# Split weights kept in DRAM from the first segment on, and a head's maximum as one row made by transposes

## The chip, the cores and the metric

The kernel runs on one core of one Trainium2 chip. The metric is the device time of one execution in microseconds, from the profiled execution and from runs timed without a profile. TensorE appears in the views as PE (matmuls) and PEld (weight loads), VectorE as DVE, ScalarE as ACT, GpSimd as POOL; a `q` behind an engine's name is its queue, from which it also issues transfers. SP is the queue that issues most of them. Sixteen DMA engines move the data.

## The reference

Two consecutive layers of a decoder trunk over 2048 tokens of width 1024, in float32. Both layers begin with an RMS norm, shifted and scaled by a condition vector, and end with a projection, a gate and a residual sum.

- Layer 0 projects to 3072 columns: four heads of a gated linear recurrence (key 128, value 128) and a causal pooling mixer with windows of 2, 4, 8 and 16, each with its own SiLU gate, then an output projection.
- Layer 1 projects to 4 x 1024 + 16 columns: queries, keys, values and gate of 16 heads of 64, and one forget logit a head. Queries and keys are RMS normed. The attention is causal with a bias of cumulative log forget values:

```
logits = q @ k.T * 64**-0.5 + cumf[:, q, None] - cumf[:, None, k]
probs  = softmax(where(causal, logits, -inf))
o      = (probs @ v) * silu(g);   x = x + gate * (o @ w_out)
```

## The kernel before

**Segments.** The 2048 tokens go in four segments of 512 (`SEG`), each through layer 0 and then layer 1, so that keys and values of earlier segments ("past chunks") are read back from DRAM. A segment has a projection stretch (layer 0, its output projection, the first projections of layer 1) and an attention stretch (16 heads, with the rest of the projections woven between).

**Precision by splitting.** A float32 operand of a matmul is split into a rounded part (type fp32r) and the remainder, and a product takes three passes (`PASSES`): high x high, high x low, low x high.

**Weights.** A weight tile is 1024 x 256. `wseq` lists the order of their use: 12 tiles of kind `a` (layer 0 in), 4 of `b` (layer 0 out), 16 of `c` (layer 1 in) and 4 of `d` (layer 1 out) in each segment, 144 uses in all, and one last tile `e` put together from parts of `d`. `prep_w(n)` loads a tile in four quarters `raw` of 256 KB (four buffers), casts each into the high half of `wt` on ACT (line 293) and subtracts into the low half, on POOL or on DVE in turn (line 294, helper line 182). This is done at every use. `wt` has two buffers, and `next_w` prepares the tile behind the one that it hands out.

**Attention operands.** For head h `prep` makes `Q1`, `Q3`, `K1` and `K2` from the transposed projection. `K1` (128 rows) holds the low and the high half of the keys. `K2` has 68 rows: 64 rows of the high half of the keys, two rows of the forget bias (high and low, from `cfd`), and two rows of ones. `Q3` has 68 rows that face these: 64 rows of queries, two of ones, and two that hold the negated maximum of each query, high and low; they begin as zeros (from `q4d`). For later segments `K1` and `K2` are stored to `k1d` and `k2d` (lines 1080 and 1081), values to `vd`.

**Maximum pass and attention.** `max_pass(s, h)` multiplies `Q3` with every chunk of `K2` and takes the maximum of each query. Past chunks come by `old_k2`, a load of 68 rows of 512 columns on SP's queue into one of three buffers (`k2o`, line 1086). At its end the maximum, four columns of 128, is negated and split by small DVE operations into eight columns (`mhl`), transposed at once to 8 rows, copied to `mr` and brought by a transfer on ACT's queue into rows 66 and 67 of `Q3` (line 1118), since a row that spans 512 columns is wanted there. `attend(s, h)` then computes, for each block of 128 keys, `pst` from `K1`, `Q1` and from `K2`, `Q3`, its exponential `ph`, the remainder `pl`, and the products with the values (`pov`, `pol`). It loads every past chunk's `K1o`, `K2o` and `Vo` itself. So every past chunk's `K2` is loaded twice for a head: once by the maximum pass, once by attention.

**Order.** `quad_attention` runs the steps of `attend` for head h in turn with those of `max_pass` for head h + 1, and calls `prep` for head h + 2 behind them; `weave` puts steps of the remaining projections (`quad_fill`) between. Instructions are put on the engines' queues by priority, which follows the program's order, and each queue runs in its order. In `prep_w` casts and subtractions are put back by 80 in priority.

Of the kernel before, what the change touches and what calls it, by code (L numbers as in the profile page):

```python
# [8 lines left out]
F32 = mybir.dt.float32  # L9
F32R = mybir.dt.float32r  # L10
BF16 = mybir.dt.bfloat16
U8 = mybir.dt.uint8
AF = mybir.ActivationFunctionType
ALU = mybir.AluOpType
# [4 lines left out]
P = 128  # L19
T = 2048  # L20
D = 1024
ND = D // P
SEG = 512
NSEG = T // SEG
NTB = SEG // P
NH = 16
HD = 64
VW = 2 * HD + 2
EPS = 1e-6
NEG = -1e30  # L30

# [2 lines left out]
def trunk(ctx, tc, x, cvec, norm_g, ada_c, ada_w, ada_b, ada_bg, lbp, w0, w0o, w1, w1f, w1o,  # L34
          onorm, poolw, pscale, foxb, qkg, out):
    nc = tc.nc
    V, S, G = nc.vector, nc.scalar, nc.gpsimd

    def mm(*a, **k):
        return nc.tensor.matmul(*a, **k)  # L40

    def transpose(o, i):
        return nc.tensor.transpose(o, i, ident[0:i.shape[0], 0:i.shape[0]])
# [5 lines left out]
    wp = E(tc.tile_pool(name="wp", bufs=2))  # L49
# [4 lines left out]
    sp = E(tc.tile_pool(name="sp", bufs=2))  # L54
    ps = E(tc.tile_pool(name="ps", bufs=2, space=PSUM))
    dr = E(tc.tile_pool(name="dr", bufs=1, space=DRAM))
# [6 lines left out]
    def small(shape, name, dt=F32):  # L63
        return sp.tile(shape, dt, name=name, tag=name)
# [22 lines left out]
    def f(ap):  # L87
        return ap.bitcast(F32)
# [32 lines left out]
    for lv in range(NL):  # L121
        half = 1 << lv
        b = 2 * half
# [26 lines left out]

    x1d = dr.tile([T, D], F32, name="x1d")
    k1d = dr.tile([NH, P, T], F32, name="k1d")
    k2d = dr.tile([NH, HD + 4, T], F32, name="k2d")
    vd = dr.tile([NH, P, T // P, VW], F32, name="vd")
    cfd = dr.tile([NH, 4, T], F32, name="cfd")
    q4d = dr.tile([4, SEG], F32, name="q4d")
    gd = dr.tile([2, D], F32, name="gd")


    def rsqrt_mean(out_t, ss, n, name):  # L160
# [101 lines left out]
    wseq = []  # L262
# [8 lines left out]
    wsrc = {"a": w0, "b": w0o, "c": w1, "d": w1o}  # L271
    grow1 = []
    wready = {}
    wpos = [0]

    def prep_w(n):
        if n >= len(wseq) or n in wready:
            return
        late = wseq[n][0] == "e"
        src = None if late else wsrc[wseq[n][0]][wseq[n][1]]  # L280
        wt = wp.tile([P, 2, ND, 256], F32R, name="wt", tag="wt")
        parts = range(3 if late else 4)
        if not late and n >= len(wseq) - 5:
            parts = range((NEARLY[wseq[n][1]] + 1) // 2)
        for h in parts:
            sl = slice(2 * h, 2 * h + 2)
            raw = wp.tile([P, 2, 256], F32, name="raw", tag="raw", bufs=4)
            nc.sync.dma_start(raw, w1o[h][:, ND - 2:, :] if late else src[:, sl, :])
            if late:
                V.tensor_tensor(raw, raw, grow1[0][:, h * 256:(h + 1) * 256].unsqueeze(1).to_broadcast([P, 2, 256]),  # L290
                                op=ALU.mult)
            tc.cur_priority += 80
            S.copy(wt[:, 0, sl, :], raw)  # L293
            split_lo(wt[:, 1, sl, :], raw, wt[:, 0, sl, :], G if (h % 2 or n == 0) and n < len(wseq) - 2 else V)
            tc.cur_priority -= 80
        wready[n] = wt

    def next_w(key, ahead=True):
# [611 lines left out]
    NEARLY = (6, 7, 7, 8)  # L910
# [65 lines left out]
    def forget_rows(s, act):  # L976
        pf = ps_pj("pfl")

        for d in range(ND):
            for b in range(2):  # L980
                mm(pf[0:48, :], wf[:, d, :], act[:, d, b, :], start=(d + b == 0), stop=(d + b == ND))
        z = tmp("z")[0:NH]
        S.activation(z, pf[0:NH, :], AF.Identity, bias=fb)
        V.tensor_tensor(z, pf[32:32 + NH, :], z, op=ALU.add)
        a = tmp("za")[0:NH]
        S.activation(a, z, AF.Abs)
        S.activation(a, a, AF.Exp, scale=-1.0)
        S.activation(a, a, AF.Ln, bias=1.0)

        V.scalar_tensor_tensor(z, z, 0.0, a, op0=ALU.min, op1=ALU.subtract)  # L990
        cf = tmp("cf")[0:NH]
        V.tensor_tensor_scan(cf, z, zero1[0:NH].to_broadcast([NH, SEG]), fcar, op0=ALU.add, op1=ALU.add)
        V.tensor_copy(fcar, cf[:, SEG - 1:SEG])
        V.tensor_scalar(cf, cf, -1.0, None, op0=ALU.mult)
        ch_ = tmp("cfh", F32R)[0:NH]
        V.tensor_copy(ch_, cf)
        cl = tmp("cfl", F32R)[0:NH]
        split_lo(cl, cf, ch_)
        nc.sync.dma_start(cfd[:, 0, s * SEG:(s + 1) * SEG], f(ch_))
        nc.sync.dma_start(cfd[:, 1, s * SEG:(s + 1) * SEG], f(cl))  # L1000

    seg1 = [dict() for _ in range(NSEG)]

# [53 lines left out]
    def prep(s, h):  # L1057

        L = seg1[s]
        qk = L["qk", h // 2]  # L1060
        j = h % 2
        pt = ps_misc("pqkT")
        for tb in range(NTB):
            transpose(pt[:, tb * P:(tb + 1) * P], qk[:, tb, j * P:(j + 1) * P])
        lo, up = slice(0, HD), slice(HD, P)
        g = col["qkg"]
        Q1 = qp.tile([P, SEG], F32R, name="Q1", tag="qa")
        Q3 = qp.tile([P, SEG], F32R, name="Q3", tag="qb")
        K1 = kp.tile([P, SEG], F32R, name="K1", tag="k1c")
        K2 = kp.tile([P, SEG], F32R, name="K2", tag="k2c")  # L1070
        S.activation(Q1[lo], pt[lo], AF.Copy, scale=g[lo])
        S.activation(K1[up], pt[up], AF.Copy, scale=g[up])
        V.scalar_tensor_tensor(Q1[up], pt[lo], g[lo], f(Q1[lo]), op0=ALU.mult, op1=ALU.subtract)
        V.scalar_tensor_tensor(K1[lo], pt[up], g[up], f(K1[up]), op0=ALU.mult, op1=ALU.subtract)
        S.copy(Q3[lo], f(Q1[lo]))
        S.copy(K2[lo], f(K1[up]))
        nc.scalar.dma_start(f(Q3[HD:HD + 4]), q4d)
        nc.scalar.dma_start(f(K2[HD:HD + 4]), cfd[h, :, s * SEG:(s + 1) * SEG])
        if s < NSEG - 1:
            nc.sync.dma_start(k1d[h, :, s * SEG:(s + 1) * SEG], f(K1))  # L1080
            nc.sync.dma_start(k2d[h, :, s * SEG:(s + 1) * SEG], f(K2[0:HD + 4]))
        L["ops", h] = (Q1, Q3, K1, K2)

    def old_k2(h, c):
        K2 = kp.tile([P, SEG], F32R, name="K2o", tag="k2o", bufs=3)
        nc.sync.dma_start(f(K2[0:HD + 4]), k2d[h, :, c * SEG:(c + 1) * SEG])
        return K2

    def max_pass(s, h):

        _, Q3, _, K2 = seg1[s]["ops", h]
        mxs = small([P, NTB, NSEG], "mxs")
        for c in range(s + 1):
            kc = K2 if c == s else old_k2(h, c)
            for i in range(NTB):
                n = SEG if c < s else (i + 1) * P
                pm = ps_mx("pmx")
                mm(pm[:, 0:n], Q3[0:HD + 4, i * P:(i + 1) * P], kc[0:HD + 4, 0:n], start=True, stop=True)
                if c < s:
                    V.tensor_reduce(mxs[:, i, c:c + 1], pm[:, 0:n], axis=AX.X, op=ALU.max)  # L1100
                else:
                    V.tensor_tensor_reduce(pm[:, 0:n], pm[:, 0:n], mq[:, SEG - n:], 1.0, NEG, op0=ALU.add,
                                           op1=ALU.max, accum_out=mxs[:, i, c:c + 1])
                if c < s or i < NTB - 1:
                    yield
        m = small([P, NTB], "m")
        V.tensor_reduce(m, mxs[:, :, 0:s + 1], axis=AX.X, op=ALU.max)
        mhl = small([P, 2, NTB], "mhl")
        mh = small([P, NTB], "mh", F32R)
        V.tensor_scalar(mh, m, -1.0, None, op0=ALU.mult)  # L1110
        V.tensor_copy(mhl[:, 0, :], f(mh))
        V.scalar_tensor_tensor(mhl[:, 1, :], m, -1.0, f(mh), op0=ALU.mult, op1=ALU.subtract)
        yield
        pt = ps_misc("pmt")
        transpose(pt[0:2 * NTB, 0:P], mhl.rearrange("p a b -> p (a b)"))
        mr = sp.tile([2 * NTB, P], F32R, name="mr", tag="mr", bufs=1)
        V.tensor_copy(mr, pt[0:2 * NTB, 0:P])
        nc.scalar.dma_start(f(Q3[HD + 2:HD + 4].rearrange("a (b t) -> a b t", t=P)), f(mr))

    def attend(s, h):  # L1120

# [2 lines left out]
        Q1, Q3, K1, K2 = L["ops", h]  # L1124
# [14 lines left out]
        for c in range(s + 1):  # L1139
            if c < s:  # L1140
                k1 = kp.tile([P, SEG], F32R, name="K1o", tag="k1o", bufs=2)
                nc.sync.dma_start(f(k1), k1d[h, :, c * SEG:(c + 1) * SEG])
                k2 = old_k2(h, c)
                vv = kp.tile([P, NTB, VW], F32R, name="Vo", tag="vo", bufs=2)
                nc.sync.dma_start(f(vv), vd[h, :, c * NTB:(c + 1) * NTB, :])
            else:
                k1, k2, vv = K1, K2, vc[:, :, j, :]
            for b in range(NTB):
                q0 = 0 if c < s else b * P
                ks = slice(b * P, (b + 1) * P)  # L1150
                st = ps_st("pst")
                mm(st[:, q0:], k1[:, ks], Q1[:, q0:], start=True, stop=False)
                mm(st[:, q0:], k2[0:HD + 4, ks], Q3[0:HD + 4, q0:], start=False, stop=(c < s))
                if c == s:
                    mm(st[:, q0:q0 + P], identb, mk, start=False, stop=True)
                ph = tmp("ph", F32R)
# [125 lines left out]
    def constants():  # L1282
# [15 lines left out]
        V.memset(o1, 1.0)  # L1298
        z1 = tmp("z1")
        V.memset(z1, 0.0)  # L1300
        nc.sync.dma_start(q4d[0:2, :], o1[0:2])
        nc.sync.dma_start(q4d[2:4, :], z1[0:2])
        for s in range(NSEG):
            nc.sync.dma_start(cfd[:, 2, s * SEG:(s + 1) * SEG], o1[0:NH])
            nc.sync.dma_start(cfd[:, 3, s * SEG:(s + 1) * SEG], o1[0:NH])
        wfr = tmp("wfr", F32, (P, ND, NH))
        nc.sync.dma_start(wfr, w1f)
        V.tensor_copy(wf[:, :, 0:NH], wfr)
# [80 lines left out]
```

## Time and profile before

| | |
|---|---|
| median of 3 runs | 3062.76 us (3058.55 to 3068.89) |
| the profiled execution | 3059.16 us |
| its span, first to last instruction | 3057.4 us |
| PE busy / DVE / ACT / POOL | 2799.8 / 2373.8 / 1792.8 / 1191.7 us |
| bytes moved by DMA | 338.56 MB, 111 GB/s in the mean |
| attention stretches | 345 to 690, 955 to 1386, 1665 to 2190, 2455 to 3041 us |

The table's times of engines are busy times over the whole span; they overlap. The stretches are given from the start of the span, and were read from the first and last matmuls of attention. The 1.8 us between span and execution lie around the first and last instruction.

### The profile page before, as it was taken

To read this page: it belongs to the slowest core of one execution; us is meant where nothing else is said; L and a number is where in the kernel's file an instruction comes from. 1 tells how busy PE (TensorE), PEld (TensorE's weight loads), DVE (VectorE), ACT (ScalarE), POOL (GpSimd) and SP (SyncE) were. 2 spreads that over 40 slices of the span, in tenths; PEclk is the share of its full clock that TensorE was granted. 3 is DMA by queue.
4 is the path that set the end of the run, shared out by engine and by line. 5 is a ranking of instruction groups with operands and counts; after the bars stand their busy time and mean duration, and the time that the engine had idled before them with its cause. 6 is when DMAs were issued, how large, how long until landed. Compare 5 with 4: busy or idle time off the path is not lost.

```text
span 3057.4 us, 49147 instructions
## 1 busy us (share of the span) xinstructions
PE 2799.8 (92%) x17020; PEld 2378.7 (78%) x17020; DVE 2373.8 (78%) x4646; ACT 1792.8 (59%) x3679; POOL 1191.7 (39%) x992
## 2 busy tenths in 40 slices
PE   4999898999998898999999899989999999999998
PEld 4888877879887777779888677777888977676767
DVE  8877688867676888876677888888758688888886
ACT  3454566763545666674445666667544566666674
POOL 3321233323212444434111555554421246655565
PEclk9999999999999999999999999999999999999999
DMA  6423454424234334434234343443333323333342
GB/s 247 163 78 104 120 141 106 122 77 128 73 114 111 101 96 109 130 90 135 68 102 118 111 108 115 117 125 106 115 99 94 110 90 101 103 96 99 92 135 79
DMA packets 198904, 338.56 MB, mean 111 GB/s; under 512 B 19768, under 2 KB 67000, under 8 KB 196096
## 3 DMA queue, kind: packets, MB, share of 16 engines
q1 hardware_dynamic: 195264, 321.52, 36.3%
q10 hardware_dynamic: 3392, 13.90, 1.3%
q8 instruction: 135, 2.21, 0.3%
q14 instruction: 113, 0.93, 0.1%
HBM read 285.72 MB, written 49.36 MB: 110 GB/s over the span
## 4 chain that ended last, share of the span: by engine, by line
PE 49%; DVE 16%; DMA 6%; ACT 5%; issue 3%; POOL 0%; SPq 0%; DVEq 0%; ACTq 0%; POOLq 0%
PE py L40 9%; PE pst L40 6%; PE pgt L40 6%; PE pqk L40 6%; PE pv L40 4%; PE pmx L40 3%; DMA K2o<-k2d 3%; PE pov L40 3%; PE pol L40 2%; PE pq L40 2%; DVE pl L182 2%; PE pl L40 2%; PE pf L40 2%; DVE wt L182 2%; DMA Q<-mr 2%
## 5 line engine op out<-in xcount | busy, mean ns | idle before, releaser
L182 POOL TENSOR_TENSOR wt<-raw,wt 128x512 fp32r<-128x512 f32 x287 | 431.3, 1511 | 998.1 <-ACT wt L293 931.9
L1168 POOL TENSOR_TENSOR la<-la,ph 128x512 f32<-128x512 f32 (+3 forms) x528 | 614.6, 1164 | 445.4 <-ACT ph L1157 396.5
L1157 ACT ACTIVATE ph<-pst 128x512 fp32r<-128x512 f32 (+3 forms) x640 | 341.6, 534 | 277.6 <-PE pst L40 258.6
L182 DVE TENSOR_TENSOR pl<-pst,ph 128x512 fp32r<-128x512 f32 (+3 forms) x640 | 385.7, 604 | 123.2 <-ACT pst L1158 111.1
L40 PE MATMUL pqk<-wt,h 128*128 128x256 f32 x3072 | 457.4, 286 | 5.7 <-DVE h L495 2.6
L40 PEld LDWEIGHTS pqk<-wt,h 128*128 128x128 f32 x3072 | 426.4, 192 | 29.8 <-DVE h L495 3.4
L40 PE MATMUL pgt<-h,wt 128*128 128x512 f32 x1536 | 418.5, 406 | 0.2 <-ACT e L527 0.2
L293 ACT CAST wt<-raw 128x512 fp32r<-128x512 f32 x578 | 337.3, 622 | 72.2 <-PE py L40 33.3
L40 PE MATMUL pv<-wt,h 128*128 128x256 f32 x2304 | 346.9, 295 | 6.0 <-DVE h L182 4.3
L40 PEld LDWEIGHTS pv<-wt,h 128*128 128x128 f32 x2304 | 324.1, 200 | 22.7 <-DVE h L182 6.4
L1158 ACT ACTIVATE pst<-pst 128x512 f32<-128x512 f32 (+3 forms) x640 | 340.1, 531 | 0.0
L40 PEld LDWEIGHTS pgt<-h,wt 128*128 128x128 f32 x1536 | 290.4, 194 | 62.0 <-issue 1.9
L182 DVE TENSOR_TENSOR wt<-raw,wt 128x512 fp32r<-128x512 f32 x291 | 264.2, 912 | 54.7 <-ACT wt L293 53.2
L1100 DVE TENSOR_REDUCE mxs<-pmx 128x1 f32<-128x512 f32 x384 | 258.4, 685 | 46.9 <-PE pmx L40 43.4
L40 PE MATMUL py<-wt,o 128*128 128x256 f32 x1536 | 203.6, 287 | 1.3 <-ACT o L1204 1.2
L40 PE MATMUL py<-wt,mix 128*128 128x256 f32 x1536 | 198.4, 287 | 3.0 <-DVE yt L842 2.1
L40 PEld LDWEIGHTS py<-wt,o 128*128 128x128 f32 x1536 | 194.2, 193 | 7.0 <-ACT o L1204 1.5
L40 PEld LDWEIGHTS py<-wt,mix 128*128 128x128 f32 x1536 | 187.7, 191 | 10.7 <-issue 4.5
L40 PE MATMUL pst<-Q,K2o 68*128 68x512 f32 x384 | 150.2, 412 | 39.6 <-DMA Q<-mr 23.0
L40 PE MATMUL pst<-Q,K1o 128*128 128x512 f32 x384 | 161.9, 427 | 18.8 <-DVE pl L182 18.2
L40 PE MATMUL pov<-ph,Vo 128*128 128x512 f32 x384 | 164.5, 428 | 4.4 <-ACT ph L1157 2.9
L40 PE MATMUL pst<-Q,K 128*128 128x512 f32 (+7 forms) x512 | 131.8, 335 | 37.1 <-DVE pl L182 27.9
(254 smaller groups left out, 5307.4 us busy)
## 6 DMA issues: line engine op xcount, KB each, us to landing
raw<-in_w_dram SPq DMA_DIRECT2D x448, 256.0 KB
K2o<-k2d SPq DMA_DIRECT2D x192, 136.0 KB
Vo<-vd SPq DMA_DIRECT2D x96, 260.0 KB
K1o<-k1d SPq DMA_DIRECT2D x96, 256.0 KB
raw<-in_w1o_dram SPq DMA_DIRECT2D x66, 256.0 KB
raw<-in_w0o_dram SPq DMA_DIRECT2D x64, 256.0 KB
vd<-Vc SPq DMA_DIRECT2D x48, 260.0 KB
ada<-in_ada_w_dram ACTq DMA_DIRECT2D x12, 1024.0 KB
```

What stands on the lines that cost most here:

```text
L40: return nc.tensor.matmul(*a, **k)
L182: (eng or V).tensor_tensor(out_t, full, f(hi), op=ALU.subtract)
L293: S.copy(wt[:, 0, sl, :], raw)
L1100: V.tensor_reduce(mxs[:, i, c:c + 1], pm[:, 0:n], axis=AX.X, op=ALU.max)
L1157: S.activation(ph[:, q0:], st[:, q0:], AF.Exp)
L1158: S.activation(st[:, q0:], st[:, q0:], AF.Exp)
L1168: G.tensor_tensor(la[:, q0:], la[:, q0:], f(ph[:, q0:]), op=ALU.add)
```

## The change

Two things are changed.

The first use of a weight tile, in the first segment, is as before, and the finished tile (high and low half, 2.1 MB) is then stored to a DRAM tensor `wd` by a transfer on ACT's queue. Every later use loads both halves from there into `wt`, 1 MB each, on SP's queue; the casts and subtractions are left out. The last uses of `d` load only the parts that are used (`NEARLY`).

The maximum of a head is no longer split into two rows. Its four columns are transposed one by one into one row of 512 columns in PSUM, and ACT writes the negated row into `Q3`. `Q3` and `K2` have 67 rows (`KR`) in place of 68: the row of the maximum (a row of ones in `K2`) stands first, the two rows of the bias behind it. `k2d`, `cfd` and `q4d` change their shape with it.

```diff
+KR = HD + 3
...
-    k2d = dr.tile([NH, HD + 4, T], F32, name="k2d")
+    k2d = dr.tile([NH, KR, T], F32, name="k2d")
...
-    cfd = dr.tile([NH, 4, T], F32, name="cfd")
-    q4d = dr.tile([4, SEG], F32, name="q4d")
+    cfd = dr.tile([NH, 3, T], F32, name="cfd")
+    q4d = dr.tile([3, SEG], F32, name="q4d")
...
+    wd = {k: dr.tile([n, P, 2, ND, 256], F32, name="wd" + k) for k, n in (("a", 12), ("b", 4), ("c", 16), ("d", 4))}
...
+        if not late and wseq[n] in wsplit:
+            kind, i = wseq[n]
+            wt = wp.tile([P, 2, ND, 256], F32R, name="wt", tag="wt")
+            nd = NEARLY[i] if n >= len(wseq) - 5 else ND
+            for b in range(2):
+                nc.sync.dma_start(f(wt[:, b, 0:nd, :]), wd[kind][i, :, b, 0:nd, :])
+            wready[n] = wt
+            return
...
-        if not late and n >= len(wseq) - 5:
-            parts = range((NEARLY[wseq[n][1]] + 1) // 2)
...
+        if not late:
+            wsplit.add(wseq[n])
+            nc.scalar.dma_start(wd[wseq[n][0]][wseq[n][1]], f(wt))
...
-        nc.scalar.dma_start(f(Q3[HD:HD + 4]), q4d)
-        nc.scalar.dma_start(f(K2[HD:HD + 4]), cfd[h, :, s * SEG:(s + 1) * SEG])
+        nc.scalar.dma_start(f(Q3[HD:KR]), q4d)
+        nc.scalar.dma_start(f(K2[HD:KR]), cfd[h, :, s * SEG:(s + 1) * SEG])
...
-            nc.sync.dma_start(k2d[h, :, s * SEG:(s + 1) * SEG], f(K2[0:HD + 4]))
+            nc.sync.dma_start(k2d[h, :, s * SEG:(s + 1) * SEG], f(K2[0:KR]))
...
-        nc.sync.dma_start(f(K2[0:HD + 4]), k2d[h, :, c * SEG:(c + 1) * SEG])
+        nc.sync.dma_start(f(K2[0:KR]), k2d[h, :, c * SEG:(c + 1) * SEG])
...
-                mm(pm[:, 0:n], Q3[0:HD + 4, i * P:(i + 1) * P], kc[0:HD + 4, 0:n], start=True, stop=True)
+                mm(pm[:, 0:n], Q3[0:KR, i * P:(i + 1) * P], kc[0:KR, 0:n], start=True, stop=True)
...
-        mhl = small([P, 2, NTB], "mhl")
-        mh = small([P, NTB], "mh", F32R)
-        V.tensor_scalar(mh, m, -1.0, None, op0=ALU.mult)
-        V.tensor_copy(mhl[:, 0, :], f(mh))
-        V.scalar_tensor_tensor(mhl[:, 1, :], m, -1.0, f(mh), op0=ALU.mult, op1=ALU.subtract)
         yield
         pt = ps_misc("pmt")
-        transpose(pt[0:2 * NTB, 0:P], mhl.rearrange("p a b -> p (a b)"))
-        mr = sp.tile([2 * NTB, P], F32R, name="mr", tag="mr", bufs=1)
-        V.tensor_copy(mr, pt[0:2 * NTB, 0:P])
-        nc.scalar.dma_start(f(Q3[HD + 2:HD + 4].rearrange("a (b t) -> a b t", t=P)), f(mr))
+        for i in range(NTB):
+            transpose(pt[0:1, i * P:(i + 1) * P], m[:, i:i + 1])
+        S.activation(Q3[HD:HD + 1], pt[0:1], AF.Copy, scale=-1.0)
...
-                mm(st[:, q0:], k2[0:HD + 4, ks], Q3[0:HD + 4, q0:], start=False, stop=(c < s))
+                mm(st[:, q0:], k2[0:KR, ks], Q3[0:KR, q0:], start=False, stop=(c < s))
```

The constant rows of `cfd` and `q4d`, written once at the start, move with the rows: three rows in place of four, and four stores fewer.

## Rows read from the trace of the kernel before

**Rows 1.** The page, busy us (share of the span) and instructions of each engine.
```profile
PE 2799.8 (92%) x17020; PEld 2378.7 (78%) x17020; DVE 2373.8 (78%) x4646; ACT 1792.8 (59%) x3679; POOL 1191.7 (39%) x992
```
**Rows 2.** The page, the chain of waits that ended last, by line.
```profile
PE py L40 9%; PE pst L40 6%; PE pgt L40 6%; PE pqk L40 6%; PE pv L40 4%; PE pmx L40 3%; DMA K2o<-k2d 3%; PE pov L40 3%; PE pol L40 2%; PE pq L40 2%; DVE pl L182 2%; PE pl L40 2%; PE pf L40 2%; DVE wt L182 2%; DMA Q<-mr 2%
```
**Rows 3.** Stages: stretch and its us, busy us by engine, PE's clock, DMA share, GB/s.
```profile
345.00:690.00 345.00, 312.54 (x2018) 270.77 (x2017) 268.90 (x578) 222.67 (x467) 106.76 (x105) 0.98 0.42 112
690.00:955.00 265.00, 255.86 (x1760) 231.55 (x1758) 183.87 (x359) 125.60 (x263) 67.18 (x48) 0.99 0.36 108
955.00:1386.00 431.00, 385.82 (x2255) 320.99 (x2256) 346.12 (x683) 280.20 (x580) 176.60 (x153) 0.96 0.40 106
...
1665.00:2190.00 525.00, 474.65 (x2631) 383.86 (x2630) 432.00 (x825) 355.72 (x721) 268.36 (x218) 0.98 0.40 112
...
2455.00:3041.00 586.00, 540.08 (x2924) 428.62 (x2923) 497.28 (x903) 390.86 (x774) 343.47 (x280) 0.98 0.33 99
```
**Rows 4.** Transfers issued in the last attention stretch, 2455 to 3041: count, KB each.
```profile
K2o<-k2d SPq DMA_DIRECT2D x93, 136.0 KB
raw<-in_w_dram SPq DMA_DIRECT2D x48, 256.0 KB
...
raw<-in_w1o_dram SPq DMA_DIRECT2D x18, 256.0 KB
```
**Rows 5.** Transfers issued in the third attention stretch, 1665 to 2190.
```profile
raw<-in_w_dram SPq DMA_DIRECT2D x64, 256.0 KB
K2o<-k2d SPq DMA_DIRECT2D x64, 136.0 KB
...
k2d<-K SPq DMA_DIRECT2D x16, 136.0 KB
```
**Rows 6.** Transfers in the second, 955 to 1386; its raw and k2d counts equal rows 5's.
```profile
K2o<-k2d SPq DMA_DIRECT2D x32, 136.0 KB
```
**Rows 7.** SP's queue in order of time: start us, us of the issue.
```profile
2616.19 0.33 SPq L1142 DMA_DIRECT2D K1o<-k1d  x1
2616.61 0.66 SPq L1086 DMA_DIRECT2D K2o<-k2d  x2
...
2624.04 0.25 SPq L1086 DMA_DIRECT2D K2o<-k2d  x1
2626.99 0.34 SPq L1142 DMA_DIRECT2D K1o<-k1d  x1
```
**Rows 8.** Two short stretches behind such issues, columns as in rows 3.
```profile
2617.50:2618.00 0.50, 0.50 (x4) 0.40 (x3) 0.49 (x2) 0.50 (x2) 0.50 (x1) 1.00 0.97 295
...
2625.34:2626.34 1.00, 1.00 (x6) 0.69 (x5) 0.73 (x2) 0.77 (x2) 0.57 (x2) 1.00 0.25 98
```
**Rows 9.** A stretch in which PE waits and the one behind it, columns as rows 3.
```profile
1000.30:1003.70 3.40, 0.73 (x4) 0.46 (x5) 3.33 (x5) 1.49 (x3) 1.99 (x2) 1.00 0.64 172
1003.80:1007.00 3.20, 3.20 (x11) 2.51 (x11) 1.66 (x3) 1.06 (x2) 0.00 (x0) 0.50 0.19 71
```
**Rows 10.** Groups of instructions on the weights: busy us, mean ns, idle before.
```profile
L182 POOL TENSOR_TENSOR wt<-raw,wt 128x512 fp32r<-128x512 f32 x287 | 431.3, 1511 | 998.1 <-ACT wt L293 931.9 <-DVE pl L182 24.3 <-DMA raw<-in_w_dram 16.2
...
L293 ACT CAST wt<-raw 128x512 fp32r<-128x512 f32 x578 | 337.3, 622 | 72.2 <-PE py L40 33.3 <-issue 9.1 <-DMA raw<-in_w_dram 8.5
...
L182 DVE TENSOR_TENSOR wt<-raw,wt 128x512 fp32r<-128x512 f32 x291 | 264.2, 912 | 54.7 <-ACT wt L293 53.2
```
**Rows 11.** Groups around the maximum row, and ACT's copy of the same length.
```profile
L1179 ACT COPY u<-pov 64x512 f32<-64x512 f32 x64 | 37.3, 583 | 33.7 <-PE pov L40 27.8 <-PE pol L40 3.0 <-DVE o L182 1.1
L1110 DVE TENSOR_SCALAR mh<-m 128x4 fp32r<-128x4 f32 x64 | 25.5, 398 | 0.9
```
**Rows 12.** Who waited for whom, whole span: us in total, times, longest us.
```profile
PE pst L40 <- DVE pl L182: 46.1, 61, 3.4
...
PE pst L40 <- DMA Q<-mr: 30.9, 14, 6.3
...
PE pst L40 <- DMA K2o<-k2d: 16.4, 19, 2.0
```

More of the change, by code (lines that the diff above doesn't have):

```diff
@@ L273, in trunk @@
     wready = {}
+    wsplit = set()
     wpos = [0]
@@ L998, in forget_rows @@
         split_lo(cl, cf, ch_)
-        nc.sync.dma_start(cfd[:, 0, s * SEG:(s + 1) * SEG], f(ch_))
-        nc.sync.dma_start(cfd[:, 1, s * SEG:(s + 1) * SEG], f(cl))
+        nc.sync.dma_start(cfd[:, 1, s * SEG:(s + 1) * SEG], f(ch_))
+        nc.sync.dma_start(cfd[:, 2, s * SEG:(s + 1) * SEG], f(cl))
     seg1 = [dict() for _ in range(NSEG)]
@@ L1300, in constants @@
         V.memset(z1, 0.0)
-        nc.sync.dma_start(q4d[0:2, :], o1[0:2])
-        nc.sync.dma_start(q4d[2:4, :], z1[0:2])
+        nc.sync.dma_start(q4d[1:3, :], o1[0:2])
+        nc.sync.dma_start(q4d[0:1, :], z1[0:1])
         for s in range(NSEG):
-            nc.sync.dma_start(cfd[:, 2, s * SEG:(s + 1) * SEG], o1[0:NH])
-            nc.sync.dma_start(cfd[:, 3, s * SEG:(s + 1) * SEG], o1[0:NH])
+            nc.sync.dma_start(cfd[:, 0, s * SEG:(s + 1) * SEG], o1[0:NH])
         wfr = tmp("wfr", F32, (P, ND, NH))
```

## The prediction

> **What bounds the kernel now.** Read first the share of busy time of each engine: TensorE (PE) is busy 92% of the span, so anything that shortens other engines can give back at most the rest [rows 1]. The chain of waits says the same in another way: its largest pieces are matmuls, but two transfers stand in it, the old key rows `K2o` (3%) and the maximum row `mr` (2%) [rows 2]. An average over the run hides where the room is, so the third view is the table by stage: a projection stretch has PE busy 255.86 of 265.00 us, while the four attention stretches leave 32 to 50 us each [rows 3]. In the projections only PE matters. In attention PE waits for others, and the loads of old keys are among those others. So the fourth view is the list of transfers in the attention stretches: each `K2o` load is 136 KB, 68 rows of 2 KB, and there are 93, 64 and 32 of them in the last three stretches, with 16 stores `k2d<-K` of the same shape in the middle ones [rows 4, 5, 6].
>
> The fifth view decides: how wide such a transfer runs. The load issued at 2624.04 is alone in flight until the next issue at 2626.99 [rows 7]. In the microsecond inside it the DMA engines are 0.25 busy and move 98 GB/s, whereas just after a 128-row `K1o` and two `K2o` loads were issued they are 0.97 busy and move 295 GB/s [rows 7, 8]. A quarter of 16 engines is four. So 68 rows go as 4 times 17 and 128 rows as 16 times 8, and one engine moves 98/4 = 24.5 GB/s, a 2 KB row in 83.6 ns.
>
> **The change part by part.**
>
> *67 rows instead of 68.* It looks like a saving of one row. But the rows above say that a transfer is cut into equal parts: with uneven parts 68 rows could have used all sixteen engines with at most five rows each, and they did not. 68 has the equal parts 1, 2 and 4 up to sixteen, and four was used. 67 is prime: one part, one engine. The other reading, that a part holds up to 17 rows, would leave 67 rows on four engines and cost nothing; it does not explain why 128 rows take sixteen engines and not eight. I take one engine, and keep zero cost as the other end. In a sentence that the rest can do without: the Trainium skill, "DMA: Bandwidth & Descriptors", section "Why a DMA increments its semaphore by 16 and not by 1", states this as a rule, the largest number of engines up to 16 that divides the slowest dimension of both sides, with 127 partitions on one engine as its example; by it the sum is the one below, by the up-to-17 reading it would be the 2995 us of the first rival, and the quarter share of the trace agrees with the rule.
>
> One `K2o` load then takes 67 x 83.6 ns = 5.60 us of a single engine instead of 17 x 83.6 ns = 1.42 us of four. That one engine also carries its sixteenth of everything else. Its work in the last attention stretch: now a mean engine is busy 0.33 x 586 = 193 us [rows 3], of which `K2o` is 93 x 68 x 0.0836/16 = 33, leaving 160; the weights' doubled bytes add 66 x 256 KB/16/24.5 GB/s = 44; the loads are 93 x 5.60 = 521 [rows 4]. Sum 725 us in a stretch of 586: at least +139. Third stretch: 0.40 x 525 - 28 = 182, plus 43 for 64 raw loads' worth of weights, plus (64 + 16) x 5.60 = 448: 673 against 525, +148 [rows 3, 5]. Second: 0.40 x 431 - 17 = 155, plus 43, plus 48 x 5.60 = 269: 467 against 431, +36 [rows 3, 6]. If this engine never pauses, the loss is 323 us.
>
> It will pause: `K2o` has three buffers, and a load waits on SP's queue until PE has read an older one, with the `K1o`, `Vo` and weight loads queued behind it. Take the other end as no work ahead: every past chunk needs a pair of loads (one for the maximum pass of the next head, one for attention), 11.2 us, plus its part of the rest (a head's store among it), and the head's own chunk runs as now. Last stretch: 3 x (11.2 + 3.2) + 586/64 = 52.4 us a head, 838 in all, +252. Third: 2 x (11.2 + 6.5) + 525/48 = 46.3, 741, +216. Second: (11.2 + 9.0) + 431/32 = 33.7, 539, +108. Sum +576. Three buffers lie between; I take the middle, +450.
>
> *PE's clock.* After a stretch of 3.40 us in which PE was busy 0.73 us the granted clock was 0.50 for the next, that is 1.2 GHz in place of 2.4, and at that level 3.2 us do 1.6 us less work [rows 9]. 16 heads x (2 + 3) chunks with a wait in each of the last two stretches give 80 x 1.6 = 128 us if each wait brings one; PE is then often not what is waited for, so I take 50.
>
> *The weights.* Of 144 uses of a tile, 108 come after its first. They lose four casts and four subtractions each: 432 x 622 ns = 269 us of ACT, 216 x 1511 ns = 326 of POOL, 216 x 912 ns = 197 of DVE [rows 10]. This work is hidden now by matmuls, so little comes back: a projection stretch has 9 us in which PE is idle [rows 3], three of them 27; I take 10. Bytes rise from 339 MB (the table above) by about 113 (reloads at twice the size) and 75 (36 stores of 2.1 MB) to 527 MB; over sixteen engines at 24.5 GB/s that is 1340 us, 44% of the span, no bound where it is spread. If a reload is late, PE's next projection is late; a tile is asked for one tile ahead, about 14 us by 96 matmuls at 255.86/1760 us [rows 3], against 2.1 MB/392 GB/s = 5.4 us. In the first segment each store stands on ACT's queue and waits for the last subtraction on POOL (1511 ns); behind it stand the exponentials `ph` that PE waits for. At most 36 x 1.5 = 54 us, nothing where POOL is done already. The first attention stretch also has 16 stores of 67 rows on one engine (90 us) and some 20 weight stores (107) beside 0.42 x 345 = 145, which fills that engine too, though PE needs only some raw loads from it. I take +15 for both.
>
> *The maximum row.* Removed a head: four small DVE operations (398 ns the first), an issue on ACT's queue and the transfer `mr`. Added: three more transposes on PE, none larger than the one there is, and one ACT pass over 512 columns, priced by the 64x512 copy `u`, 583 ns [rows 11]. PE's matmuls waited 30.9 us in 14 of 64 heads for that transfer [rows 12]. That wait goes, but in the last three stretches a late `K2o` takes its place; only the first stretch's part, about a quarter, counts: -8.
>
> Sum: the profiled execution lasted 3059.2 us (span 3057.4; the runs' median is 3062.8, 0.1% above). 3059 + 450 + 50 + 15 - 10 - 8 = 3556; I say 3555 us, +16%.
>
> **The rivals.** *The other side: 67 rows cost nothing* (a split into uneven parts, or four engines as now). Then the maximum row's 31 us return, the projections' 10, and perhaps half of the 46 us that PE's matmuls wait for `pl` on a relieved DVE [rows 12]: about 2995 us, faster by 2%. It decides if `K2o` still lands on four engines; the quarter share speaks against it. Chance 0.06. *Late weights alone*: as above, but a reload that waits for its buffer and then 5.4 us holds PE at 36 tiles by 3 us: 3059 + 108 - 41 = 3125. The 14 us of a tile speak against it; chance 0.03, and 0.01 that gains and losses cancel. *The clock takes over*: if PE spends half of its 475 + 540 us of work in the last two stretches at 1.2 GHz [rows 3], 250 us are added to the engine's loss: 3059 + 576 + 250 = 3885. That the granted clock is 0.96 to 0.98 in the attention stretches now [rows 3] speaks against it, that it will be busy only two thirds there speaks for it: 0.09. *The queue works ahead better than I think*, near the floor: 3059 + 323 - 18 = 3364, inside my range.
>
> **How the numbers follow.** One engine bounding attention has chance 0.81, with 3364 us (floor) to 3635 + 65 for clock and stores plus as much again for landing times between dependent loads, 3765; I widen to 3330 and 3860 for the clock, which holds about 0.8 of all cases. Faster by over 0.3% (what a measurement of this kernel can tell from no change): 0.06, within: 0.01, slower: 0.93.
>
> **What would show it.** `K2o` issues as many, but in flight alone they move some 25 GB/s at a share of 0.06. Attention stretches near 505, 705 and 780 us for the last three, projection stretches within 10 us of now. PE's matmuls wait for `K2o` not 16 us [rows 12] but hundreds, and the chain of waits has `K2o` as its largest piece; `Q<-mr` is gone; the granted clock of these stretches falls below the present 0.96. I am wrong if `K2o` runs at a quarter share still, or if the time is lost in the projection stretches.

## The result, and the profile after

The changed kernel takes 3496.11 us in the median of four runs (3492.11 to 3508.53) against 3064.67 us for the kernel before: a ratio of 1.1416, 95% interval 1.1379 to 1.1454. The forecast was 3555 us, slower.

The page of the changed kernel, first the busy time of each engine, then the chain of waits by line (its line numbers are up to 15 higher than before):

```profile
PE 2926.6 (84%) x17212; PEld 2488.3 (71%) x17212; DVE 2063.8 (59%) x4172; ACT 1615.7 (46%) x3312; POOL 846.7 (24%) x779
...
DMA packets 171129, 525.26 MB, mean 150 GB/s; under 512 B 15863, under 2 KB 62583, under 8 KB 136846
...
PE 54%; DMA 25%; DVE 9%; ACT 6%; issue 2%; SPq 1%; POOL 0%; ACTq 0%; DVEq 0%; POOLq 0%
DMA K2o<-k2d 18%; PE py L41 9%; PE pgt L41 7%; PE pqk L41 7%; PE pst L41 6%; PE pv L41 4%; PE pmx L41 4%; PE pl L41 2%; PE pov L41 2%; PE pu L41 2%; PE pf L41 2%; PE pq L41 2%; PE pol L41 2%; DMA vd<-Vc 1%; PE pL L41 1%
```

DVE, ACT and POOL have 177 to 345 us less work than before [rows 1], as the change meant, and PE's share of busy time falls from 92% to 84%: the work went, and waiting took its place. `K2o` was 3% of the chain [rows 2] and is now its largest piece.

The stages, with the same margins around the first and last attention matmul as in [rows 3] and with the same columns, show where:

```profile
363.00:761.00 398.00, 335.17 (x2091) 288.64 (x2091) 253.40 (x512) 225.65 (x472) 93.98 (x99) 0.93 0.59 193
761.00:1028.00 267.00, 257.74 (x1769) 233.10 (x1768) 151.07 (x336) 99.49 (x209) 21.64 (x18) 0.98 0.52 189
1028.00:1478.00 450.00, 392.40 (x2299) 328.39 (x2299) 285.81 (x579) 252.11 (x521) 124.30 (x117) 0.94 0.44 142
1478.00:1752.00 274.00, 266.13 (x1835) 241.50 (x1834) 149.01 (x343) 97.36 (x205) 12.55 (x12) 0.99 0.49 176
1752.00:2428.00 676.00, 507.19 (x2678) 411.08 (x2678) 377.32 (x720) 326.66 (x660) 205.69 (x181) 0.85 0.36 117
2428.00:2688.00 260.00, 251.79 (x1742) 227.88 (x1743) 138.58 (x319) 89.96 (x191) 12.78 (x12) 0.99 0.47 173
2688.00:3474.00 786.00, 605.82 (x2966) 486.48 (x2964) 445.83 (x800) 368.16 (x721) 293.53 (x249) 0.85 0.29 96
```

The four attention stretches were 345, 431, 525 and 586 us and are 398, 450, 676 and 786: +53, +19, +151 and +200. The first one begins 18 us later. The projection stretches hardly move. In the two longest stretches the DMA engines are busy 0.36 and 0.29 of the time, less than before, and still DMA is what PE waits for. A mean over sixteen engines cannot show one that is full.

The list of who waited for whom (us, times, longest):

```profile
ACT ph L1164 <- PE pst L41: 678.8, 294, 26.7
...
PE pst L41 <- DMA K2o<-k2d: 275.4, 53, 17.5
...
PE pmx L41 <- DMA K2o<-k2d: 48.2, 10, 18.3
```

PE's matmuls waited 16.4 us for `K2o` before [rows 12]. ACT's wait for scores to take the exponential of was 259 us in the trace of the kernel before and is 679 us now; the more is, for the most part, the same wait handed on.

How wide such a load runs now: SP's queue around three of them (the third is issued at 2710.74, and nothing else until 2720.44), and then four stretches, each of the first three as long as one load and the last behind them.

```profile
2694.74 16.22 SPq L1099 DMA_DIRECT2D K2o<-k2d  x3
2720.44 0.35 SPq L1149 DMA_DIRECT2D K1o<-k1d  x1
```
```profile
2703.33:2708.69 5.36, 0.00 (x0) 0.00 (x0) 0.00 (x0) 0.00 (x0) 0.00 (x0) 0.85 0.07 26
2708.70:2714.05 5.35, 1.86 (x4) 1.16 (x4) 1.29 (x2) 2.09 (x4) 1.26 (x1) 0.50 0.06 25
2714.06:2719.43 5.37, 4.91 (x15) 4.06 (x16) 1.98 (x3) 1.49 (x3) 0.17 (x1) 0.50 0.07 26
2719.50:2720.40 0.90, 0.90 (x5) 0.80 (x4) 0.76 (x2) 0.11 (x1) 0.90 (x1) 0.50 0.00 0
```

For 16 us the sixteen engines are 0.06 to 0.07 busy and move 25 to 26 GB/s: one engine in sixteen, at the rate of one engine in [rows 8]. In the trace's records of single packets the three loads follow each other without a gap, 67 rows each, one row every 80 ns, 5.37 us a load. Two loads were in flight at a time and the share did not rise, so they went through the same engine. The granted clock behind the first of these stretches, in which PE did nothing, is 0.50, that is 1.2 GHz.

The longest pieces of the chain of waits in order of time, in one stretch of the last segment (start us, us, what):

```profile
2981.78 18.44 DMA K2o<-k2d
3000.26 1.65 PE pst L41 x3
3001.91 3.88 PE pqk L41 x24
3009.73 9.03 DMA K2o<-k2d
3018.80 1.22 PE pst L41 x2
3022.40 7.74 DMA K2o<-k2d
```

Waits of 7.7 us and more for loads follow each other, with short pieces of PE between. One load moves in 5.37 us, so a step of 18.44 us is a load that had others ahead of it.

### The profile page after: what moved, and what is told of

It reads as the page before. It is cut to its first block, busy times and chain, and to the rows that moved or that the text cites. A ratio compares the mean times of both kernels' runs of the same rounds, so it can differ in the third digit from the quotient of the medians.

```text
span 3490.4 us, 47623 instructions
## 1 busy us (share of the span) xinstructions
PE 2926.6 (84%) x17212; PEld 2488.3 (71%) x17212; DVE 2063.8 (59%) x4172; ACT 1615.7 (46%) x3312; POOL 846.7 (24%) x779
## 4 chain that ended last, share of the span: by engine, by line
PE 54%; DMA 25%; DVE 9%; ACT 6%; issue 2%; SPq 1%; POOL 0%; ACTq 0%; DVEq 0%; POOLq 0%
DMA K2o<-k2d 18%; PE py L41 9%; PE pgt L41 7%; PE pqk L41 7%; PE pst L41 6%; PE pv L41 4%; PE pmx L41 4%; PE pl L41 2%; PE pov L41 2%; PE pu L41 2%; PE pf L41 2%; PE pq L41 2%; PE pol L41 2%; DMA vd<-Vc 1%; PE pL L41 1%
## 5 line engine op out<-in xcount | busy, mean ns | idle before, releaser
L1175 POOL TENSOR_TENSOR la<-la,ph 128x512 f32<-128x512 f32 (+3 forms) x528 | 593.0, 1123 | 1021.8 <-ACT ph L1164 963.5
L41 PEld LDWEIGHTS pqk<-wt,h 128*128 128x128 f32 x3072 | 441.7, 204 | 33.0 <-DVE xo L856 3.2
L41 PE MATMUL pst<-Q,K2o 67*128 67x512 f32 x384 | 181.9, 482 | 275.6 <-DMA K2o<-k2d 275.4
L41 PEld LDWEIGHTS pv<-wt,h 128*128 128x128 f32 x2304 | 333.9, 205 | 23.9 <-DVE h L185 4.2
L41 PEld LDWEIGHTS pgt<-h,wt 128*128 128x128 f32 x1536 | 299.4, 199 | 68.7 <-issue 2.4
L41 PEld LDWEIGHTS pst<-Q,K2o 67*128 67x128 f32 x384 | 84.2, 224 | 305.8 <-DMA K2o<-k2d 274.4
L41 PE MATMUL pmx<-K2o,Q 67*128 67x512 f32 x384 | 181.6, 480 | 67.4 <-DMA K2o<-k2d 48.2
L1173 POOL TENSOR_TENSOR la<-ph 128x512 f32<-128x512 f32 x48 | 63.5, 1322 | 606.6 <-ACT ph L1164 490.4
L185 POOL TENSOR_TENSOR wt<-raw,wt 128x512 fp32r<-128x512 f32 x74 | 106.9, 1451 | 342.6 <-ACT wt L303 282.9
L41 PE MATMUL pov<-ph,Vo 128*128 128x512 f32 x384 | 175.3, 457 | 2.5 <-ACT ph L1164 2.3
```

The source lines that it names most:

```text
L185: (eng or V).tensor_tensor(out_t, full, f(hi), op=ALU.subtract)
L1173: G.tensor_tensor(la, first, f(ph), op=ALU.add)
L1175: G.tensor_tensor(la[:, q0:], la[:, q0:], f(ph[:, q0:]), op=ALU.add)
```

## The experiments

Theory: 67 rows go through one DMA engine, and that engine bounds attention. Rivals: the weights' doubled bytes cost the time; or the maximum row does, with its three more transposes and its pass on ACT's queue.

**Rows68: only the 67 undone.**

```diff
-    k2d = dr.tile([NH, KR, T], F32, name="k2d")
-    cfd = dr.tile([NH, 3, T], F32, name="cfd")
+    k2d = dr.tile([NH, HD + 4, T], F32, name="k2d")
+    cfd = dr.tile([NH, 4, T], F32, name="cfd")
...
-        nc.sync.dma_start(f(K2[0:KR]), k2d[h, :, c * SEG:(c + 1) * SEG])
+        nc.sync.dma_start(f(K2[0:HD + 4]), k2d[h, :, c * SEG:(c + 1) * SEG])
```

The store to `k2d` and the load from `cfd` are widened alike, and `cfd` gets a fourth row of ones; the matmuls still read 67 rows.

> The changed kernel with K2 and its DRAM copy moved as 68 rows again (the 68th a row of ones that no matmul reads); weights and maximum row stay as changed. One-engine theory: the three later attention stretches lost about 370 us to loads on one DMA engine, and most of it returns: 3060 to 3140 us, with K2o alone at a DMA share of 0.25. Rival, the weights' doubled bytes cost the time: within 1% of the changed kernel, about 3480. Rival, the maximum row by transposes and an ACT pass costs it: also about 3480.

Measured: 3047.38 us, ratio to before 0.9943 (0.9919 to 0.9968). That is 13 us below its range. One row more gives back 449 us and makes the kernel 0.6% faster than before. Its attention stretches:

```profile
366.00:750.00 384.00, 332.30 (x2084) 286.38 (x2084) 252.33 (x510) 224.42 (x470) 93.38 (x99) 0.94 0.61 201
...
1018.00:1416.00 398.00, 379.38 (x2312) 317.97 (x2311) 289.62 (x581) 252.96 (x523) 123.25 (x117) 0.99 0.52 160
1690.00:2220.00 530.00, 483.34 (x2687) 392.38 (x2686) 377.91 (x724) 325.93 (x660) 206.50 (x181) 0.95 0.49 150
2480.00:3033.00 553.00, 529.76 (x2968) 427.24 (x2967) 441.81 (x799) 366.95 (x722) 296.35 (x249) 0.99 0.41 136
```

Against the changed kernel the attention stretches are 14, 52, 146 and 233 us shorter. Against the kernel before the first is 39 us longer, the third 5 us longer, and the second and the last are 33 us shorter each: that is what the rest of the change does once the row count is out of the way.

**Weights_only and max_row_67, max_row_68: each half by itself.** The first is the kernel before with the `wd` parts of the change; the others are the kernel with all of the change but those, with transfers of 67 and of 68 rows.

> The kernel before with the stored weights alone (68 rows, maximum row by transfer as before). One-engine theory: 3040 to 3130 us; what it loses lies in the first segment (stores of 2.1 MB), where the changed kernel lost 70 us. Rival, weights: 3400 or more.

Measured: 3145.11 us, 1.0257 (1.0227 to 1.0287). Not the loss of the whole change, but more than expected by the theory. The first matmul on a past chunk, which opens the second attention stretch, begins at 1040 us against 955 before, so 85 us are lost by then; behind it gains and losses nearly cancel. One loss shows in the waits of this kernel:

```profile
PE pst L40 <- DMA Q<-mr: 108.3, 40, 7.6
...
PE pst L40 <- DMA K2o<-k2d: 17.8, 22, 3.9
```

The small transfer that brings the maximum row is waited for 40 times and 108 us, against 14 times and 31 us [rows 12]. It is 4 KB, and now travels beside weight loads of 1 MB. By the trace's records of single packets its last packet has moved 3.7 us after the start of its issue (median of 64), against 1.4 us in the kernel before: 4.5 us in the 38 cases where 8 KB packets, the size in which the weights travel, move in the first microsecond, 1.5 us in the other 26.

> The kernel before with the maximum row alone, as changed (67 rows); weights are split at every use as before. One-engine theory: 3380 to 3480 us, the later attention stretches as long as in the changed kernel or a little longer, since DVE and ACT keep the splitting. Rival, weights: 3030 to 3070.

Measured: 3389.32 us, 1.1055 (1.1027 to 1.1083). With no stored weights at all most of the loss is there, 328 of 431 us.

> The maximum row alone, with K2 moved as 68 rows. One-engine theory: the wait for the small transfer goes (31 us of PE's matmul waits) and nothing takes its place: 3020 to 3060 us. Rival, the transposes and the ACT pass cost the time: above 3100.

Measured: 3040.07 us, 0.9923 (0.9893 to 0.9952). The 68th row is worth 349 us here, without stored weights. The maximum row by transposes is a small gain by itself; both rivals fall as the main cause. The two halves are not independent, though: stored weights cost 84 us beside the transfer `mr` (3145 against 3061 for the kernel before, measured beside it) and 7 us beside the transposes (3047 against 3040), no more than the runs of each scatter.

**Load67, load74, load80: the dose.** Three kernels that differ in the rows of a load alone. In all of them the stores are cut, so that they no longer sit on one engine:

```diff
-            nc.sync.dma_start(k2d[h, :, s * SEG:(s + 1) * SEG], f(K2[0:KR]))
+            nc.sync.dma_start(k2d[h * KR:h * KR + HD, s * SEG:(s + 1) * SEG], f(K2[0:HD]))
+            nc.sync.dma_start(k2d[h * KR + HD:(h + 1) * KR, s * SEG:(s + 1) * SEG], f(K2[HD:KR]))
...
-        nc.sync.dma_start(f(K2[0:KR]), k2d[h, :, c * SEG:(c + 1) * SEG])
+        nc.sync.dma_start(f(K2[0:R]), k2d[h * KR:h * KR + R, c * SEG:(c + 1) * SEG])
```

with `R` 67, 74 or 80; `k2d` is one list of rows here, with 16 rows of ones at its end, and the rows above 67 belong to the next head (or are these ones) and are not read by a matmul.

> The changed kernel with the stores to k2d cut into 64 and 3 rows; the loads keep 67 rows. One-engine theory: the last stretch (no stores) stays near 772 us, the third (653 before this edit) falls by up to 16 x 5.6 = 90 us, the second and first by 0 to 40: 3380 to 3460 us. Rival, only loads count: 3480 to 3500.

> As load67, but each load takes 74 rows (seven more, unread, of the next head). 74 has the equal parts 1 and 2 up to sixteen: two engines, 37 rows, 3.1 us. One-engine theory: the last stretch needs 204 + 93 x 3.1 = 492 us of such an engine, less than the 538 us that it takes with 68 rows, so the bound is gone and only landing times stay: 3040 to 3130 us, K2o alone at a share of 0.12. Rival, what matters is the bytes or rows moved: slower than load67. Rival, only an odd or prime number of rows is slow: the same as load80.

> As load67, with 80 rows: sixteen engines, five rows each, 0.42 us. One-engine theory: the fastest of the three, 3000 to 3045 us, below the 3047 of the kernel with 68 rows, since K2o lands over 1 us earlier. Rival, bytes: slowest of the three.

Measured: 3374.03, 3170.05 and 3023.64 us (1.102, 1.0342 and 0.9872 of before; the intervals reach 0.006 to either side at most). More rows and more bytes are faster. A stretch inside a lone load, with 74, 68 and 80 rows in this order (load74, rows68, load80):

```profile
2909.57:2911.57 2.00, 1.98 (x9) 1.65 (x10) 1.76 (x4) 0.00 (x0) 0.00 (x1) 1.00 0.13 49
```
```profile
2613.96:2614.76 0.80, 0.80 (x6) 0.70 (x6) 0.80 (x3) 0.80 (x3) 0.70 (x2) 1.00 0.26 100
```
```profile
2862.35:2862.65 0.30, 0.30 (x4) 0.28 (x4) 0.30 (x2) 0.30 (x2) 0.27 (x1) 1.00 0.93 328
```

Shares of 0.13, 0.26 and 0.93, beside the 0.07 of 67 rows, are two, four, nearly sixteen and one engine, at 25 GB/s (the last one 22) each: the equal parts of the four numbers. The rival that only an odd or prime number of rows is slow falls with 74, an even one, which lies between.

The last attention stretch of load67, load74 and load80:

```profile
2570.00:3353.00 783.00, 603.86 (x2972) 484.46 (x2971) 445.55 (x800) 368.09 (x721) 294.13 (x249) 0.85 0.29 96
```
```profile
2517.00:3157.00 640.00, 563.03 (x2971) 451.17 (x2971) 445.32 (x800) 367.29 (x722) 294.12 (x249) 0.94 0.36 119
```
```profile
2469.00:3009.00 540.00, 524.94 (x2977) 425.72 (x2976) 442.30 (x801) 367.14 (x722) 297.54 (x249) 1.00 0.44 144
```

783, 640 and 540 us for loads of 5.60, 3.09 and 0.42 us by the prediction's 83.6 ns a row. Load74 missed its expectation of 3040 to 3130: two engines are not full (an estimate of 492 us of work in 640), and still 100 us are lost against load80. So time is lost well before an engine is full. The reason is argued from the program and not shown by a run of its own: a load starts only when PE has read an older buffer, and from there its length counts. The clock is in it too: at 0.94 in place of 1.00 PE is busy 38 us longer with the same matmuls. Over the whole range a microsecond more of a load costs (783 - 540)/(5.60 - 0.42) = 47 us in a stretch with 93 loads, an estimate of half of each load's length. Load67 in turn came out 6 us below its range: cutting the stores alone was worth 122 us (3496 to 3374).

**Rows68_store_sp: the first segment.** Rows68 still has a first attention stretch of 384 us against 345. In it each finished weight tile is stored from ACT's queue, and the store's own line in rows68 shows ACT's queue standing before some of them (ns min/median/max): half hardly wait, the longest wait is 5.07 us, in which ACT does nothing else. The 35 waits sum to 29 us, 15 of them in the first attention stretch.

```profile
L308 ACTq EVENT_SEMAPHORE  x35: 17/17/5071, 44.2 to 784.5; - x35
```

```diff
-            nc.scalar.dma_start(wd[wseq[n][0]][wseq[n][1]], f(wt))
+            nc.sync.dma_start(wd[wseq[n][0]][wseq[n][1]], f(wt))
```

> The kernel with 68 rows, the stores of the split weights issued from SP's queue in place of ACT's. It asks why the first segment is 60 us longer than in the kernel before. If ACT is held by the wait for the last subtraction: 3000 to 3030 us. If the stores' 75 MB on the DMA engines cost it: within 10 us of 3047. If SP is held in the same way with loads behind it: above 3060.

Measured: 2997.08 us, 0.9785 (0.9741 to 0.983), 3 us below its first range. First the stretch, then the waits of SP's queue for the same stores:

```profile
353.00:699.00 346.00, 311.91 (x2005) 267.39 (x2004) 246.14 (x498) 219.20 (x460) 93.29 (x98) 0.98 0.68 215
```
```profile
SPq L308 <- POOL wt L185: 52.8, 20, 8.9
...
SPq L308 <- DVE wt L185: 14.3, 11, 5.2
```

The stretch is 346 us, as in the kernel before, with the same stores: 15 of the 36 are issued in it, some 31 of 75 MB. It begins at 353 us, 8 later than before. Now SP stands for the stores, 67 us in all, and it can. So the queue that issues the store was the cost, and the bytes no more than the 9 us that are left. How ACT's queue cost 51 us is shown less well: its waits (29 us) and its 36 issues (13 us) come to 42. The granted clock of the stretch is also 0.94 with the stores on ACT's queue and 0.98 without, and with the queue the order of the transfers changes; no run takes these apart.

**Load80_store_sp and max_row_80: the version that beats both.** Load80 with its stores on SP's queue, and load80 without stored weights.

> Both mends together: loads of 80 rows on sixteen engines and the stores of the weights on SP's queue. If the two losses are separate things, their gains over the kernel with 68 rows (24 and 50 us) add: 2960 to 2990 us, the shortest so far. If the stores on SP's queue hold up the loads, or both mends ease the same wait: 2985 to 3010.

> The maximum row alone with loads of 80 rows; weights are split at every use as before. Against the other kernel of this pair it tells what the stored weights are worth once neither the row count nor the ACT queue spoils them. If the stored weights are worth nothing because PE is the bound: within 10 us of the other. If they relieve the attention stretches: 3015 to 3040, some 40 us above the other.

Measured: 2976.40 us, 0.9717 (0.9696 to 0.9738), and 3030.09 us, 0.9892 (0.9875 to 0.991). The gains add as expected to the fastest kernel of this study, 2.8% below the one before and 15% below the changed one. The stored weights are worth 54 us in it, more than the 40 expected. The page of load80_store_sp:

```profile
PE 2783.6 (94%) x17212; PEld 2376.6 (80%) x17212; DVE 2063.3 (69%) x4172; ACT 1614.0 (54%) x3312; POOL 854.8 (29%) x779
...
DMA packets 177497, 530.52 MB, mean 178 GB/s; under 512 B 19671, under 2 KB 66391, under 8 KB 143214
```

It moves 5 MB more than the changed kernel, and PE is busy 94%.

## Why the prediction was right

- **67 rows on one engine.** Shown: a share of 0.07 and 25 GB/s in place of a quarter and 98, and 449 us back for one row more. A load measured 5.37 us, where 5.60 was predicted.
- **The size of it.** Predicted +450, from +323 (the engine never pauses) to +576 (no work ahead). Rows68 against the changed kernel gives 442 us between the two profiled spans, 431 of them in the last three stretches: 52, 146 and 233, where the middle of the two ends was 72, 182 and 196. These 431 us hold the clock's part too, so loads alone cost less than the 450, and the closeness of the two sums is partly luck. By the predicted work (467, 673 and 725 us) the engine would be over-full in the second stretch (450 us), which cannot be. With 5.37 us a load and the DMA shares of the changed kernel's stages the estimate is 440 of 450, 646 of 676 and 696 of 786 us: nearly full twice, 89% in the last. No view shows one engine by itself.
- **The clock, +50.** The granted clock in the last two stretches fell from 0.98 to 0.85, and PE's busy time is 115 us higher than in rows68, which has the same matmuls. How much of this delayed the end was not tried by itself; it is within the 449 us, so loads and clock together, predicted at 500, were taken 50 us too high.
- **The first segment, +15.** Mis-sized. The start and the first stretch lost 71 us (18 + 53). With 68 rows 60 of them stay, and with the stores on SP's queue nearly all go. I had a mechanism, ACT held by a store that waits for the last subtraction, and its bound of 54 us, but took 15 for it and the stores of 67 rows together. ACT's waits of 29 us are part of the loss; the rest stays open, as said above.
- **The weights, -10, and the maximum row, -8.** Mis-sized too. I gave the relief of DVE, ACT and POOL in attention no price, since the one engine would take it all. In rows68 two stretches are 33 us shorter than before, so the relief was there. The changed kernel's second stretch came out at 450, not near 505, which fits, but how much of that is relief was not tried.
- **The projections** were to stay within 10 us: they are 267, 274 and 260 us against 265, 279 and 265.
- **The rivals.** 67 rows at no cost: refuted. Late weights alone: weights_only lost 2.6%, by other waits than I named: 85 us before the second attention stretch, where the weights are stored from ACT's queue, and the transfer `mr` that lands late. The clock takes over: its granted level fell to 0.85 and the time stayed far below 3885, but the rival was priced too low, since half of 475 + 540 us of work at 1.2 GHz would add some 500 us, not 250. The forecast for 67 free rows, 2995 us, is nearer to rows68_store_sp than to rows68, for the store on ACT's queue was not in it.

The signs and places were right, 3555 against 3496. Most of the difference is the 50 us too much for loads and clock. The two other terms of the wrong size nearly cancelled: in rows68 the first segment costs 60 us where 15 were predicted, and the kernel is still 14 us faster than before, so the rest of the change gave back about 74 us where 18 were predicted.

## What to carry to other kernels

Before a transfer's row count is changed, find out over how many engines it is cut: a quarter share in a quiet microsecond told here that 68 rows used four engines, and the number 67 then needs no more than its divisors. A padded count can be faster than an exact one: 80 rows for 67. A transfer issued from a computing engine's queue makes that engine wait for whatever the transfer waits for (ACT stood 29 us so here); move it to a queue that has time.

## What was not expected of the hardware

- Loads need not fill an engine to cost time: with two engines at about three quarters of their time (an estimate, 492 of 640 us), the last attention stretch was 640 us against 540.
- Small transfers suffer from large ones: the 4 KB transfer `mr` was waited for 108 us in place of 31 once weights came as loads of 1 MB. The packets of weights_only fit this (4.5 us beside 8 KB packets, 1.5 us without); no run changes the size of the weight loads alone.
- Some 31 MB of stores beside all else cost nothing that could be seen in the first attention stretch (346 us against 345), at a DMA share of 0.68.
